# Powers of the state space eigenvalues: transposed on TensorE and stored as rows, instead of stored element by element

## The chip, the cores and the metric

One core of one Trainium2 chip. The metric is the device time of the whole kernel in microseconds (us), the median of several executions.

## The reference

Two transformer blocks in float32 over 256 tokens of 2048 features: attention of two kinds, a gated feed-forward part and a per-layer embedding in the first; gated linear attention, a state space part (S5), differential attention and a convolved feed-forward part in the second. The change lies in what the state space part needs of its parameters:

```python
mag = jnp.exp(dt * lam_r)
ab_r = mag * jnp.cos(dt * lam_i)          # a, one complex number
ab_i = mag * jnp.sin(dt * lam_i)          # for each of 64 groups x 64 states
...
x_r = jnp.einsum('bsgc,gpc->bsgp', ug, bb_r)
...
h = scan(h_t = a * h_(t-1) + x_t)         # over the 256 tokens
```

The kernel takes the tokens in chunks of four, and so needs b times a, a^2 and a^3 (and b itself), with the group's channels in the partitions.

## The kernel before

**The stream.** Nearly all of the work is matrix products whose weights are read once from HBM. `stream` (L448) walks over the weights in halves of 512 KB (128 partitions x 1024 floats). For each half SP issues the load `raw` (L459; four buffers, so the load of half i+4 is issued when half i is split), ScalarE casts the upper bits into `wh` (L466, taken four halves ahead of the matmuls), VectorE subtracts and leaves the lower bits in `wl` (L476, three halves ahead), and TensorE multiplies. Two kinds of job use it: WS (L526 and L530, 16 matmuls a half, four halves a job in the feed-forward part's `w_fin`) and AS (L560 to L562, 12 matmuls a half, six halves a job in `w_fout`). A WS job ends with a ScalarE copy (L441) and two VectorE steps (L442, L444) that free its bank; an AS job of `w_fout` ends with the VectorE sum of L973. In the first block's feed-forward part twelve WS jobs and four AS jobs follow each other in groups.

**Side work.** After every half `tick` (L271) advances each side generator by one stage, that is to its next `yield`; its instructions then stand in the engines' queues between those of two halves. `wait(n)` lets n ticks pass. All queues are in order, so the place in the code is the place on the engine.

**The part that is changed.** `s5_prep` (L1497) is such a generator, started before the seventh job of the first block's feed-forward part (L828). On small tiles of 128 partitions x 32 columns (partition p = state in two groups, column q = pair of groups) VectorE works out a, a^2, a^3 and a^4 (L1509 to L1546); all these tiles are slices of one slot `w` of 16 x 32 columns. Then POOL stores six of them, the real and imaginary parts of a^3, a^2 and a, into the DRAM tile `s5row` [3 powers, re | im, 32 q, 128 p] (L1548). The tile in DRAM has q before p, so each store writes 128 x 32 single floats. After that, for each quarter cq of the pairs: POOL sets 32 partitions (L1555, L1556), loads six pieces of `s5row`, each spread over 32 partitions (L1559), and 1 MB of b (L1561); after 30 ticks (8 in the later quarters) VectorE multiplies (`cmul`, L1619) and POOL stores 1 MB of the product `s5w` (L1566). What follows (L1571 to L1607) makes the kernels of the chunks in the same manner.

Of the kernel before, what the change touches and what calls it, by code (L numbers as in the profile page):

```python
# [9 lines left out]
F32 = mybir.dt.float32  # L10
# [3 lines left out]
ALU = mybir.AluOpType  # L14
# [7 lines left out]
NF1 = 44  # feature blocks of the first block's FFN  # L22
NF2 = 43  # feature blocks of the second block's FFN
CA = 4  # halves of weights whose high parts are taken ahead of their matmuls
SA = 3  # and low parts
COOL = 1  # steps from the last read of a bank to its next use
RAWB = 4  # halves of weights loaded ahead of their low parts

# columns of the constants
C_ID, C_ONE, C_BT, C_N = 0, 128, 256, 384  # L30
# columns of the small parameters
# [4 lines left out]
def _ws(a, b):  # L36
    """[K, F] twice -> halves [F/128 * K/512, 128, 4 k * (128 of a | 128 of b)]."""
    K, F = a.shape

    def blk(w):  # L40
        return w.reshape(K // 512, 4, 128, F // 128, 128).transpose(3, 0, 2, 1, 4)

    return np.concatenate([blk(a), blk(b)], axis=-1).reshape(-1, 128, 1024)


def _pairs(w):
    """[K, F] -> halves of the feature blocks taken two by two."""
    K, F = w.shape
    v = w.reshape(K, F // 256, 2, 128)
    return _ws(v[:, :, 0].reshape(K, F // 2), v[:, :, 1].reshape(K, F // 2))  # L50


def _as(w):
    """[K, N] -> halves [N/512 * K/256, 128, 2 k * 512]."""
    K, N = w.shape
    if K % 256:
        w = np.concatenate([w, np.zeros((256 - K % 256, N), w.dtype)], axis=0)
        K = w.shape[0]
    return np.ascontiguousarray(
        w.reshape(K // 256, 2, 128, N // 512, 512).transpose(3, 0, 2, 1, 4).reshape(-1, 128, 1024))  # L60
# [12 lines left out]
def layout(x, p, w_in, w_sb_out, w_ca_out, w_mix_out, rel_bias, g_mix, g_ffn, g_ple, g_final, w_ffn_in,  # L73
# [5 lines left out]
    a = {}  # L79
# [13 lines left out]
    def gp(v):  # [64 groups, 64 states] -> [(2 groups, 64 states), 32 pairs]  # L93
        return v.reshape(32, 128).T

    conv = np.concatenate([ffn_conv_w_2[0], ffn_conv_b_2], axis=0)  # [4, 11008]
# [9 lines left out]
    # bias of (key - query) laid out as [query, head, u], key - query = u - 128 - query  # L106
# [17 lines left out]
    # 16 k-tiles, their 16 columns behind 16 empty ones  # L124
# [11 lines left out]
    # four times for the four sums of the columns above, the bias in a row that they leave free  # L136
# [5 lines left out]
    # S5: b as [(4 times the same 2 groups, 16 channels), 32 pairs, re | im, (2 groups, 64 states)],  # L142
    # c and b also with the states in the partitions
# [16 lines left out]
class Flag:  # L160
    """A value on the chip and whether the program already has the instructions that write it."""
# [5 lines left out]
class Acts:  # L167
    """Stationary or moving activations, feature-major: per k [128, 256 high parts | 256 low parts]."""
# [17 lines left out]
class Build:  # L186
    NSLOT = 15

    def __init__(self, tc, d, out, es):
        self.tc, self.nc, self.d, self.out = tc, tc.nc, d, out  # L190
        pool = lambda name, bufs, **kw: es.enter_context(tc.tile_pool(name=name, bufs=bufs, **kw))  # noqa: E731
# [36 lines left out]
    def keep(self, st, key, shape):  # L228
        """st[key] = a slot that several jobs fill."""
# [25 lines left out]
    def lane(self, name, gen, width):  # L255
        """Queue side work of which `width` generators run at a time."""
# [39 lines left out]
    def table(self, func):  # L296
        """Have ScalarE's table of `func` loaded, in a set that serves the functions around it."""
# [17 lines left out]
    def hilo(self, hi, lo, src, scale=None):  # L315
        """hi, lo = the upper and the lower twelve bits of src * scale."""
# [8 lines left out]
    def open_acts(self, acts, g):  # L325
        """Take the slot of k-tiles 4 g .. 4 g + 3."""
# [10 lines left out]
    def to_acts(self, src, acts, n, scale=None, gcol=None):  # L337
        """Transpose src [128, 2 m, 512] (token-major) into k-tiles 4 n .. 4 n + 3 of acts."""
# [31 lines left out]
    def rsqrt(self, v, out, tmp):  # L370
        """out = v ** -0.5 (v [128, n] > 0), refined by a Newton step."""
# [12 lines left out]
    def norm(self, ss, r, rb=None):  # L384
        """r [128, 2] = rsqrt(mean + eps) per token, rb [128, 256] the same in each partition."""
# [9 lines left out]
    def norms(self, ssf, rf, ssx, tot, rb):  # L395
        """rf as by norm of ssf; tot = rf * rsqrt(mean + eps) of the rows that rf still has to scale, whose
        squares sum to ssx before."""
# [40 lines left out]
    def ws_sum(self, acc, out, rb=None, n=2):  # L438
        """out [128, n, 256] = (high half + low half of acc) * rb."""
# [8 lines left out]
    def stream(self, jobs):  # L448
# [4 lines left out]
        width = lambda j, ks: {"AS": 512 * len(ks), "WS": 1024, "W4": 512}[j.kind]  # noqa: E731  # L453
# [35 lines left out]
        for i, (j, idx, ks) in enumerate(halves):  # L489
# [15 lines left out]
            if j.by_m is not None:  # L505
                # few halves, all at hand: 128 tokens after the other
# [8 lines left out]
            elif j.kind == "W4":  # L515
                # 32 columns: every fourth k-tile into the same quarter of the rows
# [4 lines left out]
            else:  # L521
                for kk, k in enumerate(ks):
                    x = j.acts.at(k)
                    for f in range(2):
                        s = slice((kk * 2 + f) * 128, (kk * 2 + f) * 128 + 128)
                        hi = lambda: nc.tensor.matmul(  # noqa: E731  # L526
# [12 lines left out]
    def mm_as(self, acts, ks, wh, wl, acc, ms, first, end, low_last=False):  # L539
        """acc [128 tokens, m, 512] += the products of the k-tiles ks."""  # L540
# [24 lines left out]
    def as_job(self, w, n, acts, evac, k0=0, nk=None, before=None, kt=None):  # L565
        """512 columns of a product, token-major; the weights' k-tiles k0 .. k0 + nk - 1 of kt."""
# [6 lines left out]
    def ws_job(self, w, j, acts, evac, before=None):  # L573
        """Two blocks of 128 columns of a product, feature-major."""
# [12 lines left out]
    def more_consts(self, name, n, eng=None):  # L587
        """Constants of one part of the program; a later part's take their place."""
# [11 lines left out]
    def first(self):  # L600
# [44 lines left out]
        # token-major values: rows scaled by r  # L645
# [26 lines left out]
        def yt_out(Y, h, b, key):  # L672
            """Keep y^T of a head, and give up what no head needs any more."""
# [140 lines left out]
        # the residual, the feed-forward part, the per-layer embedding  # L814
# [78 lines left out]
        dram = lambda n, s: self.drp.tile(s, F32, tag=n, name=n)  # noqa: E731  # L893
# [9 lines left out]
    def av(self, out, V, w):  # L903
        """out [128, 256] (feature-major) = V^T w for the causal blocks of w [keys, 384]."""
# [5 lines left out]
    def softmax_exp(self, z, sm):  # L910
        """z [128, 128 | 256] -> exp(z - max), sm[:, 2:4] = the sums."""
# [7 lines left out]
    def residual(self, nxt, ss, gcol, r, rb, old):  # L919
        """Add a product to the residual, and make the next part's activations of it."""  # L920
# [15 lines left out]
    def hidden1(self, j, kl, acc, free, hid, rb):  # L936
        """silu(g) * u of feature block j."""
# [49 lines left out]
    def second(self):  # L987
# [5 lines left out]
        def ws_keep(key, j, n, acc, free, shape, func=None, idx=None):  # L993
            """Keep a feature-major product of two blocks in slot `key`."""
# [19 lines left out]
        # -- gated linear attention  # L1014
# [37 lines left out]
        def gla_head(h):  # L1052
# [37 lines left out]
            # keep queries of the key's own chunk, from the key on  # L1090
# [69 lines left out]
        # -- state space part  # L1160
        ZT = Acts(8)

        def u_evac(j, acc, free):
# [6 lines left out]
            # the tokens (chunk of 4, place) kept as (place, chunk)  # L1170
# [7 lines left out]
        # -- differential attention  # L1178
# [66 lines left out]
        # -- the branches merged  # L1245
# [83 lines left out]
        # the feed-forward part and the last norm  # L1329
# [17 lines left out]
        def fin_half(m, acc):  # L1347
            """The last columns of 128 tokens, and their norm."""
# [22 lines left out]
    def head_norm(self, b, t, w, acts, h, post):  # L1371
        """acts of head h = o * rsqrt(mean over the head's 256 features + eps) * post; o in bank b."""
# [31 lines left out]
    def hidden2(self, j, kl, acc, free, hid, rb):  # L1404
        """silu(gate) * val of feature block j, both convolved along the tokens."""
# [24 lines left out]
    def exp32(self, out, x, t1, t2, ti):  # L1430
        """out = exp(x), to the last bits of float32 (x clamped to the normal range)."""
        v = self.nc.vector
        ts = lambda o, i, a, b, p, q: v.tensor_scalar(out=o, in0=i, scalar1=a, scalar2=b, op0=p, op1=q)  # noqa: E731
# [16 lines left out]
    def sincos(self, s, c, th, t1, t2, t3):  # L1450
        """s, c = sin(th), cos(th)."""
# [17 lines left out]
        self.stt(s, t1, 1.0, ALU.add, t2, ALU.mult)  # sin(th / 2)  # L1469
# [5 lines left out]
        v.tensor_scalar(out=t1, in0=t1, scalar1=1.0, scalar2=None, op0=ALU.add)  # cos(th / 2)  # L1475
# [5 lines left out]
    def lam_prep(self):  # L1481
        """lam[:, 4] = exp(q1 k1) - exp(q2 k2) + 0.2"""
# [14 lines left out]
    def s5_prep(self):  # L1497
        """What the state space part needs of its parameters, laid into DRAM: with chunks of four tokens,
        a^k b (k < 4) carries a chunk's tokens to its last state, e_k = c f a^k (f = (a - 1) / lam) the
        last state of the chunk before to its tokens, and kern_k = e_k b the chunk's tokens to each other."""  # L1500
# [15 lines left out]
        # A4 = [ar | ar], [ai | -ai] of a^4; a itself in ar, ai  # L1516
# [6 lines left out]
        v.reciprocal(t1, t1)  # 1 / |lam|^2  # L1523
# [11 lines left out]
        # a^2, a^3, a^4  # L1535
# [11 lines left out]
        for i, t in enumerate((a3r, a3i, a2r, a2i, ar, ai)):  # L1547
# [209 lines left out]
```

## Time and profile before

| | |
|---|---|
| runs, us | 3229.62, 3236.39, 3237.60 |
| median, us | 3236.39 |
| span of the profiled execution, us | 3237.8 |
| TensorE busy in it | 3175.4 us, 98% of the span |
| VectorE, ScalarE, POOL busy | 1994.2, 1550.7, 80.9 us |
| mean granted TensorE clock | 0.992 |
| read from HBM, written | 599.74 MB, 14.25 MB |

The profiled execution has no other time than its span. "Busy" counts the time in which an engine executes something; "waited for" names who released an engine that stood idle; the granted clock is a share of TensorE's full speed. Times in the views are counted from the start of the span, and L numbers are lines of the kernel before.

### The profile page before, as it was taken

To read this page: it belongs to the slowest core of one execution; us is meant where nothing else is said; L and a number is where in the kernel's file an instruction comes from. 1 tells how busy PE (TensorE), PEld (TensorE's weight loads), DVE (VectorE), ACT (ScalarE), POOL (GpSimd) and SP (SyncE) were. 2 spreads that over 40 slices of the span, in tenths; PEclk is the share of its full clock that TensorE was granted. 3 is DMA by queue.
4 is the path that set the end of the run, shared out by engine and by line. 5 is a ranking of instruction groups with operands and counts; after the bars stand their busy time and mean duration, and the time that the engine had idled before them with its cause. 6 is when DMAs were issued, how large, how long until landed. Compare 5 with 4: busy or idle time off the path is not lost.

```text
span 3237.8 us, 43730 instructions
## 1 busy us (share of the span) xinstructions
PE 3175.4 (98%) x16906; PEld 2672.9 (83%) x16906; DVE 1994.2 (62%) x2593; ACT 1550.7 (48%) x2034; POOL 80.9 (2%) x160
## 2 busy tenths in 40 slices
PE   8999999998599999999999999999999999999998
PEld 7888888887488888888888888878888888888887
DVE  5656455566367676566655666955555766757666
ACT  6544444454244444456554345444444654545545
POOL 0000000000100100000000000100000000000000
PEclk9999999999799999999999999999999999999999
DMA  7454555556867766655564465755555565565554
GB/s 259 169 176 165 187 187 185 186 182 137 137 212 236 267 214 211 217 182 182 192 205 157 160 197 176 243 195 195 184 188 182 182 193 187 186 193 182 191 188 163
DMA packets 172991, 617.90 MB, mean 191 GB/s; under 512 B 23968, under 2 KB 24352, under 8 KB 169584
## 3 DMA queue, kind: packets, MB, share of 16 engines
q1 hardware_dynamic: 164992, 577.49, 55.9%
q0 software_dynamic: 7792, 37.64, 3.6%
q8 instruction: 132, 2.16, 0.3%
q14 instruction: 75, 0.61, 0.1%
HBM read 599.74 MB, written 14.25 MB: 190 GB/s over the span
## 4 chain that ended last, share of the span: by engine, by line
PE 97%; DMA 2%; DVE 0%; ACT 0%; issue 0%; DVEq 0%; SPq 0%; ACTq 0%
PE acc L526 28%; PE acc L560 17%; PE acc L561 17%; PE acc L562 17%; PE acc L530 14%; DMA raw<-in_w_fin 1%; DMA raw<-in_w_fout 1%; PE p L346 1%; PE p L1662 0%; PE p L1132 0%; PE p L1702 0%; PE p L906 0%; PE p L907 0%; PE p L908 0%; PE p L1705 0%; PE p L1109 0%
## 5 line engine op out<-in xcount | busy, mean ns | idle before, releaser
L476 DVE TENSOR_TENSOR wl<-raw,wh 128x1024 fp32r<-128x1024 f32 x1088 | 1321.5, 1220 | 671.3 <-PE acc L561 445.5
L466 ACT CAST wh<-raw 128x1024 fp32r<-128x1024 f32 x1088 | 1138.9, 1049 | 1177.1 <-PE acc L562 674.9
L526 PE MATMUL acc<-s,wh 128*128 128x512 f32 x3936 | 1389.3, 398 | 0.0
L530 PE MATMUL acc<-s,wl 128*128 128x256 f32 x3936 | 1093.0, 283 | 28.4 <-DVE wl L476 28.4
L560 PE MATMUL acc<-wh,s 128*128 128x512 f32 x2372 | 940.3, 396 | 11.6 <-ACT wh L466 10.9
L561 PE MATMUL acc<-wl,s 128*128 128x512 f32 x2372 | 932.2, 393 | 4.4 <-DVE wl L476 4.4
L562 PE MATMUL acc<-wh,s 128*128 128x512 f32 x2372 | 931.7, 393 | 0.0
L526 PEld LDWEIGHTS acc<-s,wh 128*128 128x128 f32 x3936 | 736.0, 189 | 166.4
L530 PEld LDWEIGHTS acc<-s,wl 128*128 128x128 f32 x3936 | 744.2, 189 | 41.0 <-DVE wl L476 29.9
L560 PEld LDWEIGHTS acc<-wh,s 128*128 128x128 f32 x2372 | 446.2, 188 | 111.6 <-ACT wh L466 11.2
L561 PEld LDWEIGHTS acc<-wl,s 128*128 128x128 f32 x2372 | 446.4, 188 | 104.5 <-DVE wl L476 6.0
L562 PEld LDWEIGHTS acc<-wh,s 128*128 128x128 f32 x2372 | 446.2, 188 | 101.1
L442 DVE TENSOR_TENSOR s<-acc,s 128x512 f32<-128x512 f32 (+1 forms) x120 | 82.7, 690 | 292.6 <-ACT s L441 292.5
L441 ACT COPY s<-acc 128x512 f32<-128x512 f32 (+1 forms) x120 | 70.2, 585 | 202.0 <-PE acc L526 199.9
L310 ACT ACTIVATE s<-s 128x256 f32<-128x256 f32 (+4 forms) x175 | 76.6, 443 | 103.6 <-DVE s L313 38.1
L313 DVE SCALAR_TENSOR_TENSOR s<-s,conv 128x256 f32<-128x256 f32 x172 | 79.3, 482 | 3.3
L444 DVE TENSOR_TENSOR s<-s,rb 128x512 f32<-128x512 f32 (+1 forms) x104 | 71.7, 689 | 3.5
L319 DVE TENSOR_TENSOR s<-s,s 128x256 fp32r<-128x256 f32 (+1 forms) x104 | 47.3, 458 | 23.1 <-ACT s L318 23.1
L1619 DVE TENSOR_TENSOR s<-s,s 128x1024 f32<-128x1024 f32 x48 | 58.5, 1218 | 0.0
L310 ACT ACTIVATE s<-s,conv 128x256 f32<-128x256 f32 x86 | 47.1, 595 | 22.0 <-DVE s L444 22.0
L310 ACT ACTIVATE junk<-big 128x512 f32<-128x512 f32 x48 | 30.3, 631 | 50.4 <-DVE big L925 35.5
L318 ACT CAST s<-s 128x256 fp32r<-128x256 f32 (+1 forms) x104 | 45.2, 439 | 17.5 <-DVE s L1396 8.3
(262 smaller groups left out, 1042.7 us busy)
## 6 DMA issues: line engine op xcount, KB each, us to landing
raw<-in_w_fin SPq DMA_DIRECT2D x176, 512.0 KB, 4.2
raw<-in_w_up SPq DMA_DIRECT2D x172, 512.0 KB, 3.9
raw<-in_w_fout SPq DMA_DIRECT2D x88, 512.0 KB, 4.2
raw<-in_w_down SPq DMA_DIRECT2D x84, 512.0 KB, 4.0
raw<-in_w_qksb SPq DMA_DIRECT2D x32, 512.0 KB, 3.4
raw<-in_w_qkca SPq DMA_DIRECT2D x32, 512.0 KB, 3.3
raw<-in_w_gsb SPq DMA_DIRECT2D x32, 512.0 KB, 3.4
raw<-in_w_gca SPq DMA_DIRECT2D x32, 512.0 KB, 3.4
```

Of the source, the lines that this page charges most:

```text
L310: self.nc.scalar.activation(out, in_, func, scale=scale, **kw)
L313: self.nc.vector.scalar_tensor_tensor(out=out, in0=in0, scalar=scalar, in1=in1, op0=op0, op1=op1)
L441: nc.scalar.copy(out, acc[:, 0:n, 256:512])
L442: nc.vector.tensor_add(out, acc[:, 0:n, 0:256], out)
L444: nc.vector.tensor_mul(out, out, rb.tile[:, None, :].to_broadcast([128, n, 256]) if n > 1 else rb.tile[:, None, :])
L466: nc.scalar.copy(wh[:, :n] if j.kind != "W4" else wh[:, :n].bitcast(F32), raws[i][:, :n])
L476: nc.vector.tensor_sub(wl[:, :n], r[:, :n], wh[:, :n].bitcast(F32))
L526: hi = lambda: nc.tensor.matmul( # noqa: E731 acc[:, f, :], lhsT=wh[:, s], rhs=x, start=k == first, stop=k == end)
L530: nc.tensor.matmul(acc[:, f, 256:512], lhsT=wl[:, s], rhs=x[:, 0:256], start=False, stop=False)
L560: nc.tensor.matmul(acc[:, m, :], lhsT=xl, rhs=wh[:, s], start=k == first, stop=False)
L561: nc.tensor.matmul(acc[:, m, :], lhsT=xh, rhs=wl[:, s], start=False, stop=False)
L562: nc.tensor.matmul(acc[:, m, :], lhsT=xh, rhs=wh[:, s], start=False, stop=k == end)
```

## The change

Instead of the six stores, TensorE transposes three pieces of `w`, each four neighbouring tiles wide (128 x 128), into one PSUM bank, ScalarE copies 128 x 384 of it into SBUF as `R`, and POOL stores four pieces of R, whose partitions are now (part, q) and whose columns are p: two of 64 partitions for a^3 and a^2 (real and imaginary part together), two of 32 partitions for the parts of a. Each partition of such a piece is one row of 512 bytes in `s5row`. The piece (2) holds tiles 2 to 5 (a^2, a^3), the piece (1) begins with tile 1 (the real part of a), the piece (10) ends with tile 13 (the imaginary part). The slot `tmp`, whose second half takes R, is fetched before `rows` and `B` and not after them. The generator waits three ticks ahead of the transposes and has one `yield` behind them and one behind the copy, so all that comes after it in `s5_prep` stands five ticks later. The other lines of the diff only drop comments, and no instruction comes of them; lines behind L1547 of the kernel before are 11 higher in the changed kernel at the rows shown below.

```diff
-        for i, t in enumerate((a3r, a3i, a2r, a2i, ar, ai)):
-            gp.dma_start(out=self.s5row[i // 2, i % 2].rearrange("q p -> p q"), in_=t)
+        tmp = yield from self.gslot([128, 2, 1024])
+        yield from self.wait(3)
+        b = yield from self.bank()
+        for i, o in enumerate((2, 1, 10)):
+            nc.tensor.transpose(b[0][:, i * 128:i * 128 + 128], w[0][:, o:o + 4, :].rearrange("p a q -> p (a q)"), self.ident)
+        yield
+        R = tmp[0][:, 1, 0:384]
+        nc.scalar.copy(R, b[0][:, 0:384])
+        self.unbank(b)
+        yield
+        for k, r, src in ((0, None, R[64:128, 0:128]), (1, None, R[0:64, 0:128]), (2, 0, R[0:32, 128:256]), (2, 1, R[96:128, 256:384])):
+            out = self.s5row[k].rearrange("r q p -> (r q) p") if r is None else self.s5row[k, r]
+            gp.dma_start(out=out, in_=src)
         rows = yield from self.gslot([128, 2, 8, 128])
         B = yield from self.gslot([128, 8, 2, 128])
-        tmp = yield from self.gslot([128, 2, 1024])
```

On POOL's queue, at the start of the parameters' work, this stood before (`s_5864` is `w`, `s_6311` is `rows`; a DMASW semaphore is that of an earlier POOL DMA):

```order
L729 MEMSET s_1635 64x8x64 [waits DMASW0_49]
L1548 DMA s5row<-s_5864 128x32x1 [waits DVE_49] x2
L1548 DMA s5row<-s_5864 128x32x1 x4
L1555 MEMSET s_6311 32x1024 [waits PE_49]
L1556 MEMSET s_6311 32x1024
L1559 DMA s_6311<-s5row 32x1024 [waits DMASW1_49]
```

and in the changed kernel (`s_6305` is `tmp`, `s_6438` is `rows`):

```order
L729 MEMSET s_1635 64x8x64 [waits DMASW0_49]
L1560 DMA s5row<-s_6305 64x128 [waits Activation_49]
L1560 DMA s5row<-s_6305 64x128
L1560 DMA s5row<-s_6305 32x128 x2
L1566 MEMSET s_6438 32x1024 [waits PE_49]
L1567 MEMSET s_6438 32x1024
L1570 DMA s_6438<-s5row 32x1024 [waits DMASW1_49]
```

Six stores of single elements, released by VectorE, have become four stores of rows of 128 floats, released by ScalarE; what follows them is as it was.

On TensorE, between the second and the third half of the last but one WS job of its group of twelve, this stood before:

```order
L530 MATMUL acc_6355<-s_4900,wl_6283 128x256
L526 MATMUL acc_6355<-s_4900,wh_6251 128x512
L530 MATMUL acc_6355<-s_5069,wl_6325 128x256 [waits DVE_49]
L526 MATMUL acc_6355<-s_5069,wh_6281 128x512 [waits Activation_49]
L530 MATMUL acc_6355<-s_5069,wl_6325 128x256
```

and now:

```order
L530 MATMUL acc_6338<-s_4900,wl_6283 128x256
L526 MATMUL acc_6338<-s_4900,wh_6251 128x512
L1552 MATMUL p_6381<-cst,s_5864 128x128 x3
L530 MATMUL acc_6338<-s_5069,wl_6308 128x256 [waits DVE_49]
L526 MATMUL acc_6338<-s_5069,wh_6281 128x512 [waits Activation_49]
```

The three transposes stand behind the last matmul of a half and carry no wait of their own: the half before them has already waited for `wl_6283`, which VectorE writes after the last tile of `w`. On ScalarE the copy stands between two of the casts of L466.

## Prediction

> **What bounds the kernel now.** I read the page first: which engine is full, and in which slices it is not. Its row of slices of TensorE (40 slices of 81 us, busy tenths):
>
> ```profile
> PE   8999999998599999999999999999999999999998
> ```
>
> TensorE is full but for one hole, in the tenth and eleventh slice. So nothing that other engines do is worth anything unless TensorE waits for it; I then asked whom it waited for in the whole run (line waited for: us in total, times, longest):
>
> ```profile
> PE acc L530 <- DVE wl L476: 28.4, 4, 10.8
> PE acc L560 <- ACT wh L466: 10.9, 1, 10.9
> PE acc L552 <- ACT wh L466: 8.5, 1, 8.5
> PE acc L561 <- DVE wl L476: 4.4, 3, 2.3
> ```
>
> L552 is the kernel's start. The other three, 28.4 + 10.9 + 4.4 = 43.7 us, are waits for split weights. The busy time by stretches says where (stretch: length, busy PE, PEld, DVE, ACT, POOL with instructions, granted clock, DMA share, GB/s):
>
> ```profile
> 740.00:780.00 40.00, 40.00 (x230) 34.85 (x229) 34.99 (x112) 21.53 (x28) 0.00 (x0) 1.00 0.51 169
> 780.00:800.00 20.00, 18.79 (x107) 16.04 (x106) 10.28 (x25) 4.67 (x7) 5.09 (x3) 1.00 0.70 83
> 800.00:820.00 20.00, 5.90 (x24) 4.58 (x22) 1.56 (x2) 1.35 (x2) 3.38 (x2) 0.69 0.97 57
> 820.00:840.00 20.00, 6.88 (x21) 5.66 (x22) 3.75 (x4) 2.57 (x3) 5.49 (x7) 0.59 0.91 62
> 840.00:860.00 20.00, 8.01 (x26) 5.85 (x24) 1.99 (x4) 2.72 (x4) 1.56 (x3) 0.61 0.82 92
> 860.00:880.00 20.00, 16.72 (x66) 12.88 (x65) 12.15 (x13) 10.10 (x12) 0.00 (x0) 0.91 0.75 265
> ```
>
> From 800 to 860 all compute engines are idle together while the DMA engines are 82% to 97% busy and move a third of the usual bytes. The stream of weights starves. What is in flight there, by POOL's timeline (start, duration):
>
> ```profile
> 781.84 5.09 POOL L1548 DMA_DIRECT2D s5row<-s  x3 [645.03 <-DVE s L1543]
> ...
> 825.52 1.69 POOL L1548 DMA_DIRECT2D s5row<-s  x1 [6.65 <-issue]
> 829.03 1.52 POOL L1559 DMA_DIRECT2D s<-s5row  x3
> 853.68 0.49 POOL L1559 DMA_DIRECT2D s<-s5row  x1 [10.07 <-DMA s5row<-s]
> ```
>
> and by the DMA issues (number, KB each, median us to landing), first on the page for the whole run:
>
> ```profile
> raw<-in_w_fin SPq DMA_DIRECT2D x176, 512.0 KB, 4.2
> ```
>
> then between 780 and 860:
>
> ```profile
> raw<-in_w_fin SPq DMA_DIRECT2D x5, 512.0 KB, 23.1
> raw<-in_w_fout SPq DMA_DIRECT2D x5, 512.0 KB, 35.0
> s5row<-s POOLq DMA_DIRECT2D x6, 16.0 KB, 28.5
> ```
>
> A weight half that lands in 4.2 us takes 23 and 35 here, and 16 KB of `s5row` take 28.5. The hole opens when the halves loaded ahead are used up, and closes when the last element store has landed (the load at 853.68 is released by it). The stall belongs to the six element stores.
>
> **What the stall costs.** Idle time alone misses the matmuls that ran slowly after each pause, so I measure from the end of one undisturbed job to the end of another. The copy of L441 starts when a WS job ends, the sum of L973 when an AS job ends:
>
> ```profile
> 774.60 0.59 ACT L441 COPY s<-acc 128x512 f32<-128x512 f32 x1 [1.73 <-PE acc L526]
> 785.85 0.59 ACT L441 COPY s<-acc 128x512 f32<-128x512 f32 x1 [0.60 <-PE acc L526]
> 835.23 0.58 ACT L441 COPY s<-acc 128x512 f32<-128x512 f32 x1
> 866.18 0.57 ACT L441 COPY s<-acc 128x512 f32<-128x512 f32 x1
> ```
>
> ```profile
> 879.25 1.22 DVE L973 TENSOR_TENSOR big<-big,acc 128x1024 f32<-128x1024 f32 x1 [1.70 <-PE acc L562]
> 895.91 1.22 DVE L973 TENSOR_TENSOR big<-big,acc 128x1024 f32<-128x1024 f32 x1 [1.75 <-PE acc L562]
> ```
>
> A WS job lasts 785.85 - 774.60 = 11.25 us, an AS job 895.91 - 879.25 = 16.66. From 785.85 to 879.25 lie two WS jobs (their late copies are the rows at 835.23 and 866.18) and one AS job: 2 x 11.25 + 16.66 = 39.16 us of work in 93.40. The stall costs **54.2 us**. A second count gives nearly the same: 43.7 idle, and the work lost while busy at a lower clock, 5.90 x 0.31 + 6.88 x 0.41 + 8.01 x 0.39 + 16.72 x 0.09 = 9.3; together 53.0. I take 54.2, since it is read from ends of work. The slow stretch after a pause looks like this:
>
> ```profile
> 811.19 0.58 PE L530 MATMUL acc<-s,wl 128*128 128x256 f32 x1 [9.85 <-DVE wl L476]
> 811.57 0.63 PE L526 MATMUL acc<-s,wh 128*128 128x512 f32 x1
> ...
> 814.65 0.40 PE L526 MATMUL acc<-s,wh 128*128 128x512 f32 x1
> ```
>
> An L526 takes 0.63 us right after the pause and 0.40 three us later. The Trainium skill (TensorE: Matmul & The Clock Gate, Part 1) has the clock at half for about 3.4 us after an idle window of that length. Its rule costs 1.7 us a pause; at most the five waits of L530 and L560 are such pauses, an estimate of 8.5 us, so the stall would be 43.7 + 8.5 = 52.2 at most and the new span 3186.0 at least. The trace has the slow stretch as the rule says it, and its own 54.2 decides.
>
> **The change part by part.** *Removed:* six element stores and the stall. *Added on TensorE:* three transposes; the nearest row, the same operation on the same shape, and the copy's nearest row:
>
> ```profile
> L346 PE MATMUL p<-cst,big 128*128 128x128 f32 x128 | 16.6, 272 | 0.0
> L755 ACT COPY s<-p 128x384 f32<-128x384 f32 x8 | 3.8, 478 | 0.0
> ```
>
> 16.6 us over 128 is 0.13 us of TensorE each (272 ns counts the overlap), so 3 x 0.13 = **0.4 us** on the path. They bring no wait: the order shows them without one, behind a half whose `wl` VectorE writes after the last tile of `w`. *ScalarE:* one copy of 0.48 us between two casts that run four halves (some 11 us) ahead of their matmuls, so it costs nothing; with that cover gone it would be 0.5 us. *POOL:* four stores of 16 or 32 KB in place of six. No row shows stores of 512-byte rows. From above they are bounded by the element stores' 28.5 us, from below by the nearest small transfer, 64 KB in 256 pieces of 256 bytes:
>
> ```profile
> s<-s SPq DMA_DIRECT2D x16, 64.0 KB, 5.6
> ```
>
> None of TensorE's waits belongs to those sixteen. The four stores hold 192 rows in all, nearer to this row than to the 4096 elements of one store before, so I take 5.6 us each and nothing for TensorE. *Moved:* everything of `s5_prep` behind this point comes five ticks (5 x 2.81 = 14 us) later in the work: POOL's memsets, the loads of `s5row` and of b, the multiplications. SP's weight loads are not moved past anything. *What is late next:* with the stall gone, the six loads of 128 KB and the 1 MB of b, which ran into the end of the stall, fall at about 800 us into the full stream. The second quarter of `s5_prep` shows what that costs:
>
> ```profile
> 951.35 2.92 POOL L1559 DMA_DIRECT2D s<-s5row  x6
> 954.26 0.57 POOL L1561 DMA_DIRECT2D s<-in_s5b  x1
> ```
>
> ```profile
> 960.00:965.00 5.00, 5.00 (x31) 4.40 (x30) 0.88 (x1) 0.00 (x0) 0.00 (x0) 1.00 0.98 388
> ```
>
> These are the same loads beside the same stream, and TensorE is busy 5.00 of 5.00 us. The cover is the halves split ahead. I cost the burst at 0, which is also its lower bound, since TensorE waits for nothing there that could end. Its upper bound is the tail of the present stall, where the same loads ran with empty buffers. The first AS job began here:
>
> ```profile
> 853.89 0.79 PE L560 MATMUL acc<-wh,s 128*128 128x512 f32 x1 [10.87 <-ACT wh L466]
> ```
>
> and ended at 879.25: 25.4 us for 16.7, so **8.7 us**.
>
> *Sum:* 3237.8 - 54.2 + 0.4 = 3184.0 us of span. The profiled span lies 1.4 above the median of the runs (3236.39), so the time is **3182.6 us**.
>
> **The rivals.**
>
> *The burst collides* (0.08). As above, with the loads five ticks nearer to the start of the AS jobs: 3182.6 + 8.7 = 3191.3. Against it: three of four quarters pass without a wait.
>
> *Only half of the stall is the stores'* (0.04). From 829 on, loads of `s5row` are in flight too. What was lost by then, from the stretches above: 20 - 18.79 = 1.2, then 20 - 5.90 x 0.69 = 15.9, then 9 of 20 us of 20 - 6.88 x 0.59 = 15.9, which is 7.2; together 24.3. If the loads made the rest, the time would be 3237.8 - 24.3 + 0.4 - 1.4 = 3212.5. For it: the overlap. Against it: the same loads are harmless at 951. Beside it stands a rule that speaks against this change: the Trainium skill (DMA: Bandwidth & Descriptors, Anatomy of one DMA) prices a POOL transfer at 2.0 us plus its bytes at 436 GB/s, an estimate of 12 us for six of 16 KB; by it the stores would make 12 us of the stall at most. The 28.5 us of the trace contradicts it for single elements.
>
> *The stores do nothing better* (0.01). If DRAM took rows as badly as elements, or the stall had another cause, the time stays at 3236.
>
> *Slower: the row stores land too late for VectorE* (0.01). The first multiplication stood 30 ticks behind the stores. Its row (times, first and last start):
>
> ```profile
> L1619 DVE TENSOR_TENSOR s<-s,s x48: 1215/1218/1226, 919.0 to 1296.5; 128x1024 f32<-128x1024 f32 x48
> ```
>
> and the landing of the element stores:
>
> ```profile
> DMA to landing us min/median/max: 22.8/28.5/40.0
> ```
>
> In the changed kernel it is due at 919.0 - 54.2 + 14 = 879, the first store at 782 + 14 = 796. VectorE waits in order, and the splits of all later weights are queued behind it; three halves (8.4 us) are split ahead. If four stores took 40.0 us each, one after the other, they would land at 956: 956 - 879 - 8.4 = 69 us of stall in place of 54, and 3182.6 + 69 = 3251. It decides only beyond some 145 us from the first store to the last landing.
>
> **How the numbers follow.** The forecast has 0.86. Range: below, the fastest of the runs lies 6.8 us under the median, 3182.6 - 6.8 = 3176; above, the burst's bound and as much as the highest run lies over the median, 3191.3 + 1.2, so 3193. That leaves out the last three cases, 0.06. About 0.3% (9.7 us) can be told from no change: forecast, burst and half stall are faster by more, 0.98; the fourth is the same, 0.01; the last is slower, 0.01.
>
> **What would show it.** Right: no wait of TensorE for L466 or L476 about 780 to 880, DMA at some 170 to 200 GB/s there and weight halves landing in about 4 us, three transposes of 0.27 us near 791 without idle time before them, four short stores near 796, the clock at 1.00. Wrong: waits of TensorE between 796 and 830 while the loads of `s5row` and b land (the burst), a store that lands in over 20 us, or a wait of VectorE at its first multiplication near 879.

## The result, and the profile after

The changed kernel takes 3182.88 us (median of 4 runs, 3182.23 to 3183.52), the kernel before beside it 3236.66 (4 runs, 3229.62 to 3237.6). The ratio of the times is 0.9843, with a 95% interval of 0.9829 to 0.9857: 53.8 us, or 1.6%, faster. The forecast of 3182.6 lies 0.3 us from the measured time.

The page of the changed kernel has the same row of slices for TensorE (tenths of busy time in 40 slices), without the hole:

```profile
PE   8999999999999999999999999999999999999998
```

TensorE's waits in the whole run (line waited for: us in total, times, longest). The waits for `wl` are gone, and of those for `wh` only the one at the kernel's start is left. The 0.8 us at L560 are a wait for a sum of the residual stream at the kernel's end, which the kernel before has too.

```profile
PE acc L552 <- ACT wh L466: 8.6, 1, 8.6
PE acc L560 <- DVE big L1351: 0.8, 1, 0.8
```

The stretches that starved before (length, busy time of PE, PEld, DVE, ACT and POOL with instructions, granted clock, DMA share, GB/s):

```profile
780.00:800.00 20.00, 20.00 (x117) 17.44 (x116) 14.87 (x31) 10.12 (x15) 6.45 (x12) 1.00 0.76 229
800.00:820.00 20.00, 20.00 (x100) 16.76 (x99) 12.16 (x15) 9.55 (x12) 0.94 (x2) 1.00 0.84 279
820.00:840.00 20.00, 20.00 (x88) 16.27 (x87) 10.16 (x9) 7.87 (x8) 0.00 (x0) 1.00 0.59 194
840.00:860.00 20.00, 20.00 (x88) 16.27 (x87) 10.21 (x9) 7.38 (x7) 0.00 (x0) 1.00 0.58 184
```

TensorE is busy 20.00 of 20.00 us in each, at a clock of 1.00. Between 800 and 860 the DMA engines spend less of their time (0.58 to 0.84, before 0.82 to 0.97) and move two to five times the bytes (184 to 279 GB/s, before 57 to 92). The DMA issues between 780 and 860 (number, KB each, median us to landing):

```profile
raw<-in_w_fout SPq DMA_DIRECT2D x24, 512.0 KB, 4.2
raw<-in_w_fin SPq DMA_DIRECT2D x6, 512.0 KB, 4.3
s<-in_s5b POOLq DMA_DIRECT2D x1, 1024.0 KB, 7.7
s<-s5row POOLq DMA_DIRECT2D x6, 128.0 KB, 3.7
s5row<-s POOLq DMA_DIRECT2D x2, 32.0 KB, 4.1
s5row<-s POOLq DMA_DIRECT2D x2, 16.0 KB, 3.5
```

A weight half lands in 4.2 to 4.3 us again, where it took 23 to 35, and a row store in 3.5 to 4.1, where an element store took 28.5. POOL's own timeline (start, duration, idle time before and its releaser):

```profile
792.97 2.06 POOL L1560 DMA_DIRECT2D s5row<-s  x4 [656.50 <-ACT s L1555]
795.08 0.96 POOL L1566 MEMSET s<- 32x1024 f32 x1
795.97 0.95 POOL L1567 MEMSET s<- 32x1024 f32 x1
797.46 2.92 POOL L1570 DMA_DIRECT2D s<-s5row  x6 [0.54 <-DMA s5row<-s]
800.37 0.56 POOL L1572 DMA_DIRECT2D s<-in_s5b  x1
```

From the first store to the issue of b POOL now needs 8 us; before, it was over 70. Between the two anchors of the prediction, the copy that ends a WS job and the sum that ends an AS job, now lie

```profile
785.56 0.59 ACT L441 COPY s<-acc 128x512 f32<-128x512 f32 x1 [0.73 <-PE acc L526]
```

```profile
824.99 1.22 DVE L973 TENSOR_TENSOR big<-big,acc 128x1024 f32<-128x1024 f32 x1 [1.74 <-PE acc L562]
```

824.99 - 785.56 = 39.43 us, for work that was put at 39.16 without the transposes; before it was 93.40. So 54.0 us left the place that the prediction named.

### The profile page after: what moved, and what is told of

It reads as the page before. It is cut to its first block, busy times and chain, and to the rows that moved or that the text cites. A ratio compares the mean times of both kernels' runs of the same rounds, so it can differ in the third digit from the quotient of the medians.

```text
span 3180.2 us, 43735 instructions
## 1 busy us (share of the span) xinstructions
PE 3161.4 (99%) x16909; PEld 2668.2 (84%) x16909; DVE 1994.4 (63%) x2593; ACT 1553.3 (49%) x2035; POOL 72.5 (2%) x158
## 4 chain that ended last, share of the span: by engine, by line
PE 99%; ACT 0%; DMA 0%; DVE 0%; DVEq 0%; issue 0%; SPq 0%; ACTq 0%
PE acc L526 29%; PE acc L560 17%; PE acc L562 17%; PE acc L561 17%; PE acc L530 15%; PE p L346 1%; PE p L1673 0%; PE p L1132 0%; PE p L1713 0%; PE p L906 0%; PE p L908 0%; PE p L907 0%; PE p L1716 0%; PE p L1109 0%; PE p L1128 0%; PE p L1707 0%
## 5 line engine op out<-in xcount | busy, mean ns | idle before, releaser
L466 ACT CAST wh<-raw 128x1024 fp32r<-128x1024 f32 x1088 | 1138.9, 1049 | 1110.3 <-PE acc L562 672.1
L560 PE MATMUL acc<-wh,s 128*128 128x512 f32 x2372 | 939.0, 396 | 0.8 <-DVE big L1351 0.8
L560 PEld LDWEIGHTS acc<-wh,s 128*128 128x128 f32 x2372 | 445.9, 188 | 99.2 <-issue 1.7
```

What stands on the lines that cost most here:

```text
L466: nc.scalar.copy(wh[:, :n] if j.kind != "W4" else wh[:, :n].bitcast(F32), raws[i][:, :n])
L560: nc.tensor.matmul(acc[:, m, :], lhsT=xl, rhs=wh[:, s], start=k == first, stop=False)
```

## The experiments

The theory: the element stores alone make the stall, because single elements in DRAM slow every other transfer. Rivals: the overlap with the loads of `s5row` and b makes half of it; it is the place in the order; it is the number of stores or their bytes; it is single elements as work of the DMA engines, wherever they go. Times are medians with their range; each ratio is to the kernel before, run on the same chip beside it, whose median was 3230.34 us (e1 to e4), 3226.62 (e5, e6, e7, e9), 3228.2 (e8, e10, e11) and 3226.71 (e12). The changed kernel itself was timed only with the result; "over the changed kernel" is against its 3182.88. "Cover" is what has been loaded and split ahead of the matmuls when a stall begins, "landing" the time from the issue of a transfer until its data are there.

**Row stores undone, the rest of the change kept** (e1_elements). Only the four row stores are replaced; the transposes and the copy stay, unused:

```diff
-        for k, r, src in ((0, None, R[64:128, 0:128]), (1, None, R[0:64, 0:128]), (2, 0, R[0:32, 128:256]), (2, 1, R[96:128, 256:384])):
-            out = self.s5row[k].rearrange("r q p -> (r q) p") if r is None else self.s5row[k, r]
-            gp.dma_start(out=out, in_=src)
+        for i, t in enumerate((a3r, a3i, a2r, a2i, ar, ai)):
+            gp.dma_start(out=self.s5row[i // 2, i % 2].rearrange("q p -> p q"), in_=t)
```

> The changed kernel with its three transposes, its copy and its shift by five ticks, but the six element stores of the kernel before in the place of the four row stores (the transposed rows are made and not used). Theory, the element stores make the stall: back to 3237 us (3236.7 + 0.4), TensorE waits of 40 to 46 us that begin some 14 us later than before, after about 810. Rival, the gain comes of the new place of the work in the order: about 3183 us and no waits.

Measured: 3228.06 (3220.28 to 3238.78), ratio 0.9999 [0.9987, 1.0011]: the whole gain is gone, so it is the stores', and transposes, copy and new order bring nothing that ten runs can tell. POOL's first stores, and TensorE's waits:

```profile
782.29 5.08 POOL L1559 DMA_DIRECT2D s5row<-s  x3 [647.85 <-DVE s L1543]
```

```profile
PE acc L530 <- DVE wl L476: 20.5, 3, 10.1
PE acc L560 <- ACT wh L466: 3.7, 1, 3.7
PE acc L561 <- DVE wl L476: 2.3, 3, 1.1
```

The stores did not come 14 us later: they read `w`, POOL waits only for VectorE, and VectorE is done at 782. In this profile the waits add up to 26.5 us, not to the 40 to 46 expected, and before to 43.7; the stall varies from execution to execution (25 runs of the kernel before took 3224.92 to 3235.4 us).

**The loads behind the stores put off by 45 ticks** (e2_loads_late), and **each store 12 ticks after the one before** (e3_spaced), both in the kernel before:

```diff
         for i, t in enumerate((a3r, a3i, a2r, a2i, ar, ai)):
             gp.dma_start(out=self.s5row[i // 2, i % 2].rearrange("q p -> p q"), in_=t)
+        yield from self.wait(45)
```

> The kernel before with 45 ticks (126 us) between the six element stores and the first memsets and loads of s5row, so that no load is in flight during the stall. Theory, the stores alone make the stall: 3233 to 3238 us, TensorE waits of about 40 us between 797 and 870, none beside the loads. Rival, the loads that overlap the last stores make the second half: the loss is 24 us, 3207 us, with the waits over by about 835.

In e3 the wait stands in the loop:

```diff
         for i, t in enumerate((a3r, a3i, a2r, a2i, ar, ai)):
             gp.dma_start(out=self.s5row[i // 2, i % 2].rearrange("q p -> p q"), in_=t)
+            yield from self.wait(12)
```

> The kernel before with 12 ticks (34 us) after each of the six element stores, so that they never run beside each other. Six stores were in flight for 72 us, 12 us each, and the stream then ran at about 57 of 190 GB/s, so each would put it back by some 8 us; three to four halves (8 to 11 us) are split or loaded ahead. If the stall is a matter of crowding: 3183 to 3195 us, waits of TensorE under 12 us in all. If each element has its fixed price on the stream: 54.2 / 6 = 9 us for each store whatever the distance, 3236 us, six waits.

Measured: e2 3224.91 (3222.44 to 3231.85), ratio 0.9987 [0.9977, 0.9996]; e3 3236.09 (3229.2 to 3239.06), ratio 1.0016 [1.0006, 1.0027]. Neither edit moved what it should. In e2 the loads still follow the last store at once:

```profile
820.77 1.68 POOL L1548 DMA_DIRECT2D s5row<-s  x1 [5.07 <-issue]
824.27 1.51 POOL L1560 DMA_DIRECT2D s<-s5row  x3
```

and in e3 the first three stores still go out together:

```profile
781.56 5.08 POOL L1548 DMA_DIRECT2D s5row<-s  x3 [648.10 <-DVE s L1543]
```

A tick sets where an instruction stands among the others in the program; an engine whose queue holds little else runs it as soon as its data are there. Both are inconclusive; e6 and e5 make the same tests with data that arrive late.

**Loads held back by data** (e6_held). VectorE zeroes the tiles into which `s5row` and b are loaded, 45 ticks behind the stores, and the loads must wait for that:

```diff
         tb = tmp[0][:, 0].rearrange("p (j n) -> p j n", j=8)
+        yield from self.wait(45)
+        v.memset(rows[0], 0.0)
+        v.memset(B[0], 0.0)
         for cq in range(4):
```

> A second try at late loads: in the kernel before, VectorE sets the two slots of the loads to zero 45 ticks (126 us) after the stores, and POOL's first memsets and loads of s5row and of b have to wait for that; the six element stores stay as they were. Theory, the stores alone make the stall: 3226 to 3236 us, TensorE waits of 27 to 44 us about 797 to 860, none when the loads come. Rival, the loads that overlap the last stores make the second half: 3205 to 3212 us, waits of under 25 us.

Measured: 3227.79 (3222.87 to 3235.04), ratio 0.9999 [0.9986, 1.0012]. POOL's timeline shows the first load 129 us behind the last store, and TensorE's waits show that the stall stays where it was:

```profile
822.49 1.68 POOL L1548 DMA_DIRECT2D s5row<-s  x1 [6.89 <-issue]
...
949.39 0.95 POOL L1558 MEMSET s<- 32x1024 f32 x1 [125.21 <-DVE s L1555]
...
951.18 2.96 POOL L1562 DMA_DIRECT2D s<-s5row  x6
```

```profile
PE acc L530 <- DVE wl L476: 21.3, 3, 10.2
PE acc L560 <- ACT wh L466: 2.8, 2, 2.1
PE acc L561 <- DVE wl L476: 2.5, 2, 1.4
```

The loads themselves pass beside a full TensorE (stretches of the same kernel):

```profile
940.00:960.00 20.00, 20.00 (x117) 17.52 (x116) 12.38 (x13) 7.56 (x10) 5.31 (x9) 1.00 0.58 182
960.00:980.00 20.00, 20.00 (x117) 17.54 (x116) 13.71 (x18) 11.53 (x15) 0.00 (x0) 1.00 0.84 302
```

The rival of the half falls: stores without loads stall as in e1 (26.6 us of waits, there 26.5), loads without stores not at all.

**Stores apart** (e5_apart), in the kernel before, each from a copy that VectorE makes 12 ticks after the last:

```diff
+        tmp = yield from self.gslot([128, 2, 1024])
         for i, t in enumerate((a3r, a3i, a2r, a2i, ar, ai)):
-            gp.dma_start(out=self.s5row[i // 2, i % 2].rearrange("q p -> p q"), in_=t)
+            c = tmp[0][:, 1, 32 * i:32 * i + 32]
+            v.tensor_copy(c, t)
+            gp.dma_start(out=self.s5row[i // 2, i % 2].rearrange("q p -> p q"), in_=c)
+            yield from self.wait(12)
...
-        tmp = yield from self.gslot([128, 2, 1024])
```

> A second try at stores that stand apart, since a tick alone does not hold POOL back: each of the six element stores now reads a copy (128 x 32, on VectorE, 0.2 us) that is made 12 ticks (34 us) after the one before, so POOL must wait for it. If the stall is a matter of crowding (a lone store starves the stream for some 8 us, which the three or four halves ahead cover, and the stream catches up in the 34 us): 3183 to 3195 us, TensorE waits under 12 us in all. Rival, a store takes as long alone as in the crowd (24 to 28 us to landing, some 18 us of stream lost, 9 more than the cover): 3228 to 3238 us, six waits of about 7 to 9 us.

Measured: 3201.65 (3200.32 to 3203.72), ratio 0.9919 [0.9904, 0.9934], so 18.8 us above the changed kernel's 3182.88, between the two ranges expected. The six stores start 33 to 36 us apart (POOL's timeline, the first two) and each lands in 15 to 20 us. TensorE waits twice, at about 808 and 982, behind the first store and the last, which has the loads beside it:

```profile
785.09 1.72 POOL L1551 DMA_DIRECT2D s5row<-s  x1 [649.60 <-DVE s L1550]
821.13 1.70 POOL L1551 DMA_DIRECT2D s5row<-s  x1 [34.32 <-DVE s L1550]
```

```profile
PE acc L530 <- DVE wl L476: 7.1, 2, 3.9
```

So even one element store holds the weights back: the 20 us from 780 and from 820, each with one store, move 128 and 122 GB/s, where the changed kernel's stream alone takes 184 (its stretch from 840). The cover hides that for four of the six. The first store has no load of POOL's beside it and still leads to a wait; why is open. With the slow clock behind the two waits about 13 of the 18.8 us are accounted for; the rest stays open (some 2 to 3 us may be the same as in e4 below, which takes that much longer behind this place).

**Two element stores, the rest rows** (e7_two), in the changed kernel:

```diff
+        for i, t in enumerate((a3r, a3i)):
+            gp.dma_start(out=self.s5row[0, i].rearrange("q p -> p q"), in_=t)
-        for k, r, src in ((0, None, R[64:128, 0:128]), (1, None, R[0:64, 0:128]), (2, 0, R[0:32, 128:256]), (2, 1, R[96:128, 256:384])):
+        for k, r, src in ((1, None, R[0:64, 0:128]), (2, 0, R[0:32, 128:256]), (2, 1, R[96:128, 256:384])):
```

> The changed kernel, but a^3 goes out by two element stores (8192 elements in place of 24576), a^2 and a by rows. By elements in proportion with nothing covered: a third of 47 to 54 us, so 16 to 18 us over the changed kernel, 3199 to 3201. With the halves ahead covering the first 8 to 11 us: 5 to 10 us over it, 3188 to 3193, one or two waits of TensorE. If a pair alone goes under the cover: 3183, no wait.

Measured: 3194.74 (3194.28 to 3195.42), ratio 0.9897 [0.9881, 0.9914], 11.9 us over the changed kernel: above the 5 to 10 us expected with a cover and below the 16 to 18 without. It is a quarter, not a third, of the 44 to 54 us that six cost; a price by element from which the cover takes its part once would do that, but the run alone does not show it. TensorE's waits for `wl`:

```profile
PE acc L530 <- DVE wl L476: 9.3, 2, 8.3
```

**The same six stores in runs of 128 bytes** (e4_runs). In the kernel before, each store writes the 32 floats of a partition side by side. The values lie in DRAM in another order, so S5 works with other numbers; number, bytes and place of the stores are the same:

```diff
-            gp.dma_start(out=self.s5row[i // 2, i % 2].rearrange("q p -> p q"), in_=t)
+            gp.dma_start(out=self.s5row[i // 2, i % 2].rearrange("q p -> (q p)").rearrange("(p q) -> p q", q=32), in_=t)
```

> The kernel before with the six stores as they were in number, bytes, source and place, but each partition's 32 floats written as one run of 128 bytes; no transposes. The powers then lie in s5row in another order, so the state space part works with other numbers. Theory, it is the 4096 single elements of each store: no stall, 3183 us (3236.7 - 54.2 + 0), DMA landing in about 5 us. Rival, it is six small stores to DRAM from POOL whatever their grain: 3236 us. In between: 128-byte runs still cost something, with TensorE waits of a few us about 797.

Measured: 3184.79 (3184.71 to 3185.31), ratio 0.9859 [0.9844, 0.9874], 1.9 us from the changed kernel, with no transpose at all. Six stores of 16 KB at the same time leave no stall when they go in 128 pieces each instead of 4096 (POOL's timeline, then the landing between 780 and 860):

```profile
781.29 3.21 POOL L1548 DMA_DIRECT2D s5row<-s  x6 [648.13 <-DVE s L1543]
```

```profile
s5row<-s POOLq DMA_DIRECT2D x6, 16.0 KB, 4.3
```

Between the two anchors of the prediction, 824.45 - 785.29 = 39.16 us pass:

```profile
785.29 0.59 ACT L441 COPY s<-acc 128x512 f32<-128x512 f32 x1 [0.65 <-PE acc L526]
824.45 1.22 DVE L973 TENSOR_TENSOR big<-big,acc 128x1024 f32<-128x1024 f32 x1 [1.75 <-PE acc L562]
```

That is the prediction's figure for the work without a stall, so the 1.9 us come later in the kernel. So neither the number of stores, nor their bytes, nor their place makes the stall, but the single elements. The 128 runs of a store lie one behind the other in DRAM, as the rows of the changed kernel do; runs of this length that lie apart were not tried.

**Single elements from SBUF to SBUF** (e9_sbuf_elements), **to DRAM 8 bytes apart** (e10_dram_near), **to DRAM in pieces of 16 bytes** (e11_dram_16). The changed kernel with six more transfers of 16 KB ahead of its copy, into places that nothing reads. In e9:

```diff
+        for i, t in enumerate((a3r, a3i, a2r, a2i, ar, ai)):
+            gp.dma_start(out=tmp[0][:, 1, 384 + 64 * i:448 + 64 * i].rearrange("p (q two) -> p q two", two=2)[:, :, 0], in_=t)
```

The loop is the same in e10, and in e11 with pieces of four floats; `scr` is one more tile in DRAM, 6 x 128 x 64 floats. The line in the loop is, in this order,

```diff
+            gp.dma_start(out=self.scr[i].rearrange("p (q two) -> p q two", two=2)[:, :, 0], in_=t)
```

```diff
+            gp.dma_start(out=self.scr[i].rearrange("p (q e) -> p q e", e=8)[:, :, 0:4], in_=t.rearrange("p (q e) -> p q e", e=4))
```

> The changed kernel with six more transfers of 128 x 32 single elements from POOL, as many and as small as the element stores of before, but from SBUF to SBUF, each element to every second float of its own partition; nobody reads them. If the single elements themselves hold up the 16 DMA engines: the stall comes back in full or nearly, 3225 to 3240 us, TensorE waits of 25 to 45 us, landing in 20 to 30 us. If it is the writing of single elements to DRAM: 3183 to 3186 us, no waits, landing in about 5 us.

> The changed kernel with six more transfers of 128 x 32 single elements from POOL into a scratch tensor in DRAM, each element to every second float, so that neighbours lie 8 bytes apart and not 512; nobody reads them. If single elements written to DRAM hold up the stream wherever they lie: 3220 to 3240 us, TensorE waits of 25 to 45 us, landing in 20 to 30 us. If it was the step of 512 bytes between them: 3183 to 3190 us, waits under 5 us, as for the elements written to SBUF.

> As the run with elements 8 bytes apart in DRAM, but in pieces of four floats (16 bytes) with 16 bytes between them: the same bytes in a quarter of the pieces, 6144 in place of 24576. If the price is one per piece: a stall of a quarter, 11 to 14 us less the 8 to 11 that are covered, 3183 to 3188 us, landing in 6 to 9 us. If any piece far under 512 bytes costs as the single ones do by bytes: 3220 to 3240 us.

Measured: e9 3182.59 (3182.28 to 3182.91), ratio 0.9860 [0.9845, 0.9874], which is the changed kernel's time; e10 3280.16 (3278.88 to 3288.76), ratio 1.0166 [1.0143, 1.0189], 97 us above it; e11 3194.84 (3193.54 to 3195.71), ratio 0.9895 [0.9880, 0.9909], 12 us above it. Stretches of e9, and its elements' landing:

```profile
780.00:800.00 20.00, 20.00 (x117) 17.43 (x117) 12.13 (x27) 8.26 (x12) 10.71 (x8) 1.00 0.93 178
800.00:820.00 20.00, 19.65 (x96) 16.12 (x96) 10.85 (x13) 8.03 (x11) 6.78 (x12) 1.00 0.98 238
```

```profile
s<-s POOLq DMA_DIRECT2D x6, 16.0 KB, 10.9
```

With the same tiles as source and as many elements, the DMA engines are as busy (0.93 to 0.98), yet 178 to 238 GB/s are moved and TensorE loses 0.35 us. The expected landing of 5 us was missed. In e10 the stream breaks down, and the waits of 86.9 us in all are twice those of the kernel before, above all that was expected (one stretch, the landing, the two largest waits):

```profile
820.00:840.00 20.00, 3.45 (x15) 2.70 (x13) 0.00 (x0) 0.00 (x0) 0.00 (x0) 0.59 0.93 28
```

```profile
scr<-s POOLq DMA_DIRECT2D x6, 16.0 KB, 51.4
```

```profile
PE acc L530 <- DVE wl L476: 56.8, 3, 20.5
PE acc L560 <- ACT wh L466: 27.9, 2, 17.4
```

e9 and e10 differ only in where the elements go. It is their writing to DRAM that costs. Elements 8 bytes apart cost twice those 512 bytes apart of the kernel before (97 us against 44 to 54). In e11 the pieces are four times as long and a quarter as many, and land in

```profile
scr<-s POOLq DMA_DIRECT2D x6, 16.0 KB, 15.8
```

The 12 us lie between the two ranges expected and are an eighth of e10's 97. With e4 there are thus three points at 16 KB a store: 4096 pieces of 4 bytes stall, 1024 of 16 bytes still cost 12 us, 128 of 128 bytes nothing that can be seen. Whether length or number decides these runs do not separate.

**Single elements read from DRAM** (e12_reads), six loads in the same place of the changed kernel:

```diff
+        for i in range(6):
+            gp.dma_start(out=tmp[0][:, 1, 384 + 32 * i:416 + 32 * i], in_=d["s5bt"][:, 64 * i:64 * i + 64].rearrange("p (q two) -> p q two", two=2)[:, :, 0])
```

> The changed kernel with six more transfers of 128 x 32 single elements from POOL, now read from DRAM (every second float of an input, 8 bytes apart) into SBUF; nobody uses them. They wait only for their slot, so they may come earlier than the stores did. If single elements in DRAM hold up the stream in both directions: 3210 to 3290 us, TensorE waits of 25 to 90 us beside them. If only writing them does: 3182 to 3186 us, waits under 2 us, landing in some 10 us as for the elements written to SBUF.

Measured: 3202.32 (3198.34 to 3204.91), ratio 0.991 [0.9877, 0.9942], 19 us over the changed kernel and between the two ranges expected. The loads wait for no data but a free tile, so they went out at 564 to 597, in another part of the kernel. Their landing there, and TensorE's largest wait:

```profile
s<-in_s5bt POOLq DMA_DIRECT2D x6, 16.0 KB, 21.2
```

```profile
PE p L346 <- DVE s L798: 12.0, 1, 12.0
```

VectorE comes late to L798 because its splits stood waiting for weights. So element reads also hold up the stream; how much they would cost at 790 the run does not say, as the cover there is another one.

**A larger burst** (e8_burst): three copies of 1 MB from DRAM to DRAM (`scr` is again one more tile there) behind the row stores, read by nobody:

```diff
+        for i in range(3):
+            gp.dma_start(out=self.scr[i], in_=d["s5b"][i + 1])
```

> The changed kernel with three copies of 1 MB from DRAM to DRAM behind the four row stores on POOL's queue, so that the burst of the first quarter (1.8 MB) meets 3 MB more; nobody reads them. If the burst was near the end of its cover (a cast waited 3.4 us for its weights at 807 us): waits of TensorE, 3186 to 3200 us. If large pieces share the DMA engines evenly with the weights, which need 187 GB/s: 3183 to 3185 us and no waits.

Measured: 3184.24 (3183.84 to 3185.06), ratio 0.9862 [0.9848, 0.9877], 1.4 us over the changed kernel. Its stretch with the burst, and its one new wait:

```profile
800.00:820.00 20.00, 18.96 (x95) 15.65 (x94) 8.79 (x11) 5.72 (x8) 1.95 (x4) 1.00 0.93 311
```

```profile
PE acc L561 <- DVE wl L476: 1.0, 1, 1.0
```

Three megabytes more on top of the kernel's own burst of 1.75 MB use up the cover and 1.0 us beyond it. Large transfers beside the stream cost almost nothing; 96 KB in single elements cost 44 to 54 us.

No version beat the changed kernel. Its TensorE is busy 99% of the span, and of what the change added only the transposes are on the path.

## Why the prediction was right

**The stall belongs to the stores, and costs 54.2.** Right as to cause: with the stores put back (e1) all of the gain goes, with the loads taken out of the overlap (e6) nothing changes. Right as to size in the profiled execution: 93.40 - 39.43 = 54.0 us between the anchors. But this execution had a large stall. Reckoned in the same way, the four other profiles with the same six stores have 50.9 us (e3), 40.3 (e2), 38.0 (e6) and 37.4 (e1); in the later sessions the kernel before took 3226.62 to 3230.34, 44 to 47 us more than the changed kernel. The sum took one execution's stall against that execution's span, and that the medians beside the result also lie 53.8 us apart is luck; by these later and larger samples the gain is 44 to 47.

**The clock.** The prediction weighed its 54.2 against an estimate of 52.2 at most by the rule of the Trainium skill (TensorE: Matmul & The Clock Gate, Part 1). The 54.0 between the anchors exceed that estimate by 1.8 us, and the granted clock, 0.59 to 0.69 in the starved stretches before, is 1.00 in all of them now: the rule has the kind of the loss right, and the trace its size.

**Transposes 0.4.** They came where the order had them, without idle time before them. TensorE's timeline (start, duration) has the three on 0.25 us of path, from the start of the first to the start of the next half at 791.25, as starts overlap. Between the anchors the changed kernel has 39.43 us and e4, without transposes, 39.16; the difference of 0.27 agrees:

```profile
790.77 0.40 PE L526 MATMUL acc<-s,wh 128*128 128x512 f32 x1
791.00 0.49 PE L1552 MATMUL p<-cst,s 128*128 128x128 f32 x3
791.25 0.36 PE L530 MATMUL acc<-s,wl 128*128 128x256 f32 x1
```

**ScalarE's copy 0.** It took 0.46 us at 792.21 and delayed no matmul.

**Row stores 5.6 us each, off the path.** They land in 3.5 to 4.1 us, below the lower bound of 5.6, which was read from transfers of another kind (SBUF to SBUF, on SP's queue) and so bounded nothing; and they go out at 793, not 796. So VectorE's first multiplication is released long before it is due (878.7, forecast 879), and the slower rival had nothing to decide:

```profile
L1630 DVE TENSOR_TENSOR s<-s,s x48: 1215/1219/1226, 878.7 to 1255.1; 128x1024 f32<-128x1024 f32 x48
```

**The burst costs 0.** Right. The stretch 800 to 820 has TensorE busy 20.00 of 20.00 at 279 GB/s, and e8 shows that nearly 3 MB more would have been covered too. Its bound of 8.7 us, taken from the tail of the old stall, was the stores' own: e6 has the loads alone, and TensorE stays full.

**The rivals.** The half falls by e6. The estimate of 12 us for six stores of 16 KB by the Trainium skill (DMA: Bandwidth & Descriptors, Anatomy of one DMA) is some 2 us a store: runs and rows, with landings of 3.5 to 4.3 us, are within 2.3 us of it, and single elements with 28.5 are not. That rows might be taken as badly as elements falls by the changed kernel and by e4.

**The step from span to time, -1.4.** Wrong in sign. The changed kernel's times lie 1.8 to 2.2 us over their spans (3182.36 against 3180.2 in the profiled execution), and its span of 3180.2 is 3.8 below the 3184.0 of the sum. The span fell by 57.6 us, 54.0 of them at the stall and 0.3 ahead of it. The other 3.3 come in evenly over the 2300 us behind it (the last sum of L973 went from 3110.2 to 3052.7, that is 57.5), without any wait of TensorE, a difference of about 0.15% in rate. It does not go with the stall: from the first sum of L973 to the last, e1, which stalls, takes 2227.8 us and the changed kernel 2227.7, while e4, which does not stall, takes 2230.9 and the kernel before 2231.0. The order of the work behind the stores, which e1 shares with the changed kernel, may make it, or chance (e2, made from the kernel before, has 2228.3); that was not tried. So two small errors cancelled, and the 0.3 us between forecast and result are luck beyond some 4 us.

## What to carry to other kernels

Where all engines idle together while the DMA engines are busy and move few bytes, look for a small transfer in pieces of single elements to or from DRAM, and price it by what the stream beside it loses, not by its bytes. Give it runs: runs of 128 bytes, one behind the other, were enough here (e4), and three transposes of 0.25 us in all bought rows of 512. A stall of this sort varies from one execution to the next, so take its size from several before you forecast a gain by it.

## What the runs showed of the hardware

- Six transfers of 16 KB in 4-byte pieces: SBUF to SBUF they land in 10.9 us and cost the kernel nothing (e9); to DRAM at a step of 512 bytes 28.5 us and 44 to 54 of stall; at a step of 8 bytes 51.4 us and 97 us more for the kernel (e10). That neighbours in DRAM are worse than distant elements was not expected. The Trainium skill (DMA: Bandwidth & Descriptors, Why small descriptors are slow) says that transfers within SBUF are spared the penalty of small pieces; e9 agrees as to the kernel's time, though its 16 KB still took 10.9 us to land, where runs to DRAM took 4.3. The same page (Specifications) names 512 bytes as the least for full rate and a read-modify-write below it; here runs of 128 bytes, one behind the other, already left the stream alone, and what in DRAM or in the DMA engines makes single elements so dear is not settled.
- POOL's issue of an element store took 1.69 us, of the same bytes in 128-byte runs 0.54 (3.21 us for six in e4).
- Ticks that separate instructions in the program did not separate them in time on POOL, whose queue was otherwise empty (e2, e3); data made late did (e5, e6).
